# Seven block products in place of eight for ten pairs of row blocks of a down projection, its columns in two chunks

## The chip, the cores and the metric

One core of a Trainium2 chip runs the whole layer as one program. The metric is the device time in microseconds. Engines: PE does the matmuls (and loads their stationary operands, PEld), DVE the elementwise work on two operands, ACT copies and activations, SP issues most transfers, and POOL is all but idle here. Each engine works through its own instructions in order; they wait for each other by semaphores.

## What is computed

A layer with three attention branches and a gated MLP, in fp32, on 256 rows of 2048 columns. The part that changes is the last line, the down projection:

```python
h2 = _rmsnorm(x, ffn_norm)
u = _causal_dwconv(h2 @ w_up, conv_w, conv_b)
g, val = jnp.split(u, 2, axis=-1)
return x + (jax.nn.silu(g) * val) @ w_down    # (256 x 5504) @ (5504 x 2048)
```

## The kernel before

All weights come in the order of use as tiles of 128 x 1024 (512 KB), in an order that `weight_chunks` writes out by hand and the host packs. `w_tiles` loads a tile on SP's queue into one of four `raw` buffers (L155), rounds it on ACT to `whi` (L159) and subtracts on DVE to get the rest, `wlo` (L160); there are three buffers each of `whi` and `wlo`. The rounding and the subtraction have high priority. The order of the instructions on each engine is set by a scheduler when the program is built: what is ready first comes first, and the source order and the priority decide between what is ready. Pools hand out a buffer again when all that used it is done.

Activations are kept the same way, as a rounded part and a rest, and a product takes three matmuls: high by high, high by low, low by high. All go through `mm` (L100). The results are summed in PSUM, which has eight banks of 512 fp32 columns: pool `pj` has two tiles of two banks, pool `pa` the tiles `t`, `s` (twice) and `o` of a bank each.

The up stage goes over the 43 blocks of 128 hidden columns in pairs (the last one alone). For each pair and each half (gate, value) `proj_cols` takes 16 row blocks of `w_up`; then come the convolution on ACT and DVE, silu, the product of the halves (L820), and `split` into `fc` (L190, L192), which holds the hidden activations, transposed.

The down stage goes over `DOWN`: three chunks of 512 columns and two of 256. For each, `proj_rows` goes over the 43 row blocks of `w_down`, and for each row block over the two halves `tt` of the 256 rows, with three matmuls; the row blocks of one tile come together (two at 512 columns, four at 256). At the end of a chunk a piece of `x2d` (the residual, in DRAM) is loaded into `xr` on SP (L827), the sum is added on DVE (L828) and stored on SP's or ACT's queue (L829).

Of the kernel before, what the change touches and what calls it, by code (L numbers as in the profile page):

```python
# [11 lines left out]
F32 = mybir.dt.float32  # L12
F32R = mybir.dt.float32r
BF16 = mybir.dt.bfloat16
I32 = mybir.dt.int32
AF = mybir.ActivationFunctionType
# [3 lines left out]
P = 128  # L20
D = 2048
# [4 lines left out]
NFF = DFF // P  # L26
# [13 lines left out]
NEG = -1.0e30  # L40


DOWN = ((0, 512), (512, 512), (1024, 512), (1536, 256), (1792, 256))


def weight_chunks():

    for c in range(4):
        yield "kv", KD, c * 512, 512
    for base, n in ((QM, 1024), (KB, 1024), (QB, 1024), (VB, 512), (QI, 256), (QI + 256, 328), (VB + 512, 512)):  # L50
        for c in range(0, n, 512):
            yield "in", KD, base + c, min(512, n - c)
    for br in (2, 1, 0):
        for c in range(0, D, 512):
            yield "in", KD, GL + br * D + c, 512
            yield "b%d" % br, D // 2 // P, c, 512
        if br == 2:
            for base, n in ((KA, 256), (QA, 256), (VA, 512)):
                for c in range(0, 1024, n):
                    yield "in", KD, base + c, n  # L60
    for c in range(4):
        yield "out", KD, c * 512, 512
    for c in range(0, DFF, 256):
        for half in range(2):
            yield "up", KD, half * DFF + c, min(256, DFF - c)
    for c0, n in DOWN:
        yield "down", NFF, c0, n


def weight_tiles():  # L70
# [16 lines left out]
def hybrid_block(ctx: ExitStack, tc: tile.TileContext, x, xT, mem, memT, pos, inv, prm, gqk, bg, wts, out):  # L87
# [11 lines left out]
    def mm(o, l, r, start, stop):  # L99
        nc.tensor.matmul(o, l, r, start=start, stop=stop, skip_group_check=True)  # L100
# [44 lines left out]

    tiles = enumerate(weight_tiles())

    def w_tiles(name, nk, c0, n):

        j = 0  # L150
        while j < nk:
            at, (name_, j_, kn, c0_, n_) = next(tiles)
            assert (name_, j_, c0_, n_) == (name, j, c0, n), (name, j, c0, n)
            raw = wraw.tile([P, 1024], F32, name="raw")
            nc.sync.dma_start(raw[:, :kn * n], wts[at, :, :kn * n])  # L155
            hi = whl.tile([P, 1024], F32R, name="whi")
            lo = whl.tile([P, 1024], F32R, name="wlo")
            with tc.high_priority():
                nc.scalar.activation(hi[:, :kn * n], raw[:, :kn * n], AF.Copy)  # L159
                nc.vector.tensor_sub(lo[:, :kn * n], raw[:, :kn * n], hi[:, :kn * n].bitcast(F32))  # L160
            for k in range(kn):
                yield j + k, hi[:, k * n:(k + 1) * n], lo[:, k * n:(k + 1) * n]
            step()
            j += kn
# [625 lines left out]
        r2b = bcast_cols(const, r2, "r2b")  # L790


    with ExitStack() as fctx:
        ap_ = fctx.enter_context(tc.tile_pool(name="ap", bufs=1))
        up = fctx.enter_context(tc.tile_pool(name="up", bufs=2))
        fc = ap_.tile([P, NFF, 2, T], F32R, name="fc")
        for c0 in range(0, NFF, 2):
            nb = min(2, NFF - c0)
            conv = []
# [18 lines left out]
            g_, v_ = conv[0][:, :nb, :], conv[1][:, :nb, :]  # L818
            nc.scalar.activation(g_, g_, AF.Silu)
            nc.vector.tensor_mul(v_, g_, v_)  # L820
            split(fc[:, c0:c0 + nb], v_)

        for c0, n in DOWN:
            ps = proj_rows(fc, "down", NFF, c0, n)
            for tt in range(2):
                xr = up.tile([P, 512], F32, name="xr2")[:, :n]
                nc.sync.dma_start(xr, x2d[tt * P:(tt + 1) * P, c0:c0 + n])  # L827
                nc.vector.tensor_add(xr, xr, ps[:, tt, :n])  # L828
                (nc.sync, nc.scalar)[tt].dma_start(out[tt * P:(tt + 1) * P, c0:c0 + n], xr)  # L829


_ORDER = ["x", "xT", "mem", "memT", "pos", "inv", "prm", "gqk", "bg", "wts"]
# [39 lines left out]
```

## Time and profile before

| what | us |
|---|---|
| median of 3 runs (lowest, highest) | 1701.38 (1698.99, 1701.79) |
| the profiled execution, its own time | 1699.5 |
| the profiled execution, its span | 1697.8 |
| up stage, by the timeline of PE | 985 to 1456.4 |
| down stage, first matmul to last adds | 1456.5 to 1694.1 |

The span goes from the first to the last instruction of the profiled execution. The granted clock is 1.00 in all 40 slices of the page. Durations of matmuls overlap, since they are pipelined: their pace is read from their starts. In a row of a timeline a group of like instructions is merged (xcount), and square brackets tell how long the engine was idle before it and who released it.

### The profile page before, as it was taken

What the parts mean: (1) busy time and instruction counts of PE and PEld (TensorE: products, weight loads), DVE (VectorE), ACT (ScalarE), POOL (GpSimd) and SP (SyncE); (2) the same over time, 40 slices, a digit from 0 to 9 for tenths busy, and PEclk for the clock granted to TensorE, in tenths of its full rate; (3) what the DMA queues carried; (4) which work ended last, traced back from release to release, by engine and by line L of the source; (5) the groups of instructions that cost most, each with busy time, mean ns of one, the idle gap of its engine ahead of it and who ended that gap; (6) DMA issues with size and microseconds to landing.
All of it is one profiled execution on the core that took longest, in us unless ns stands there. A gap on an engine that the chain in (4) does not pass through costs nothing.

```text
span 1697.8 us, 22795 instructions
## 1 busy us (share of the span) xinstructions
PE 1686.8 (99%) x8658; PEld 1440.5 (85%) x8658; DVE 1071.7 (63%) x1589; ACT 863.5 (51%) x1147; POOL 6.9 (0%) x58
## 2 busy tenths in 40 slices
PE   8999999999999999999999999999999999999999
PEld 6888889888888888888888888888888888888899
DVE  6686866686554455555565577777777777644443
ACT  6555554444444477544444455555555555433432
POOL 0000000000000000000000000000000000000000
PEclk9999999999999999999999999999999999999999
DMA  9855445555565555566666665555555555565663
GB/s 329 299 186 188 144 155 180 180 186 184 176 199 190 195 174 173 183 211 203 203 203 218 218 210 190 192 190 187 193 191 187 191 193 187 193 205 204 220 205 128
DMA packets 99966, 332.80 MB, mean 196 GB/s; under 512 B 11152, under 2 KB 16656, under 8 KB 99856
## 3 DMA queue, kind: packets, MB, share of 16 engines
q1 hardware_dynamic: 98992, 330.29, 58.9%
q8 instruction: 67, 1.10, 0.2%
q10 hardware_dynamic: 864, 1.06, 0.2%
q14 instruction: 43, 0.35, 0.1%
HBM read 327.11 MB, written 4.19 MB: 195 GB/s over the span
## 4 chain that ended last, share of the span: by engine, by line
PE 99%; DMA 0%; DVE 0%; issue 0%; ACT 0%; SPq 0%; DVEq 0%
PE pj L100 95%; PE s L100 2%; PE o L100 1%; DMA raw<-in_wts 0%; PE t L554 0%; PE t L775 0%; PE t L749 0%; PE t L325 0%; PE t L676 0%; ACT whi L159 0%; DVE xf L369 0%; DVE wlo L160 0%; PE t L502 0%; DVE xc L192 0%; SPq L288 0%
## 5 line engine op out<-in xcount | busy, mean ns | idle before, releaser
L160 DVE TENSOR_TENSOR wlo<-raw,whi 128x1024 fp32r<-128x1024 f32 (+2 forms) x591 | 719.6, 1218 | 566.2 <-ACT whi L159 565.1
L159 ACT ACTIVATE whi<-raw 128x1024 fp32r<-128x1024 f32 (+2 forms) x591 | 623.3, 1055 | 778.8 <-PE pj L100 635.0
L100 PE MATMUL pj<-whi,xc 128*128 128x512 f32 (+2 forms) x1536 | 481.1, 387 | 0.5 <-DVE xc L192 0.5
L100 PE MATMUL pj<-x2c,whi 128*128 128x512 f32 x1376 | 477.4, 391 | 0.0
L100 PE MATMUL pj<-x2c,wlo 128*128 128x256 f32 x1376 | 385.5, 280 | 0.0
L100 PEld LDWEIGHTS pj<-whi,xc 128*128 128x128 f32 x1536 | 285.2, 188 | 55.3 <-DVE xc L192 1.0
L100 PEld LDWEIGHTS pj<-x2c,whi 128*128 128x128 f32 x1376 | 257.3, 187 | 56.3
L100 PE MATMUL pj<-wlo,xc 128*128 128x512 f32 (+2 forms) x768 | 293.3, 382 | 0.0
L100 PEld LDWEIGHTS pj<-x2c,wlo 128*128 128x128 f32 x1376 | 260.1, 189 | 0.0
L100 PE MATMUL pj<-whi,fc 128*128 128x512 f32 (+1 forms) x860 | 220.8, 347 | 0.0
L100 PEld LDWEIGHTS pj<-whi,fc 128*128 128x128 f32 x860 | 150.6, 189 | 20.2
L100 PEld LDWEIGHTS pj<-wlo,xc 128*128 128x128 f32 x768 | 144.6, 188 | 25.8
L100 PE MATMUL pj<-wlo,fc 128*128 128x512 f32 (+1 forms) x430 | 149.1, 347 | 0.0
L100 PEld LDWEIGHTS pj<-wlo,fc 128*128 128x128 f32 x430 | 81.4, 189 | 10.1
L100 PE MATMUL pj<-xc,whi 128*128 128x512 f32 x256 | 88.9, 394 | 0.0
L100 PE MATMUL pj<-whi,mc 128*128 128x512 f32 x256 | 81.8, 398 | 6.1 <-ACT whi L159 6.1
L100 PE MATMUL pj<-whi,mg 128*128 128x512 f32 x256 | 81.1, 393 | 0.0
L100 PE MATMUL pj<-xc,wlo 128*128 128x256 f32 x256 | 70.9, 277 | 0.0
L100 PEld LDWEIGHTS pj<-whi,mc 128*128 128x128 f32 x256 | 49.1, 192 | 16.3 <-ACT whi L159 6.3
L100 PEld LDWEIGHTS pj<-xc,whi 128*128 128x128 f32 x256 | 48.0, 188 | 11.1
L100 PEld LDWEIGHTS pj<-whi,mg 128*128 128x128 f32 x256 | 48.1, 188 | 9.8
L100 PE MATMUL pj<-wlo,mc 128*128 128x512 f32 x128 | 51.2, 400 | 0.4 <-DVE wlo L160 0.4
(222 smaller groups left out, 1297.1 us busy)
## 6 DMA issues: line engine op xcount, KB each, us to landing
raw<-in_wts SPq DMA_DIRECT2D x578, 512.0 KB, 3.3
th<-in_bg SPq DMA_DIRECT2D x24, 256.0 KB, 5.6
raw<-in_wts SPq DMA_DIRECT2D x5, 492.0 KB, 4.2
nat_rows<-in_mem SPq DMA_DIRECT2D x4, 512.0 KB, 6.5
nat_rows<-in_x SPq DMA_DIRECT2D x4, 512.0 KB, 6.9
xf<-in_xT SPq DMA_DIRECT2D x4, 512.0 KB, 5.3
xrow<-in_x SPq DMA_DIRECT2D x8, 256.0 KB, 4.4
x2d<-xrow SPq DMA_DIRECT2D x8, 256.0 KB, 4.2
```

The source lines that it names most:

```text
L100: nc.tensor.matmul(o, l, r, start=start, stop=stop, skip_group_check=True)
L159: nc.scalar.activation(hi[:, :kn * n], raw[:, :kn * n], AF.Copy)
L160: nc.vector.tensor_sub(lo[:, :kn * n], raw[:, :kn * n], hi[:, :kn * n].bitcast(F32))
```

## The change

The down projection's columns come as two chunks of 1024. Of the 43 row blocks, 20 pairs (a, b) and a tail of three blocks are taken. Ten of the pairs (`SEVEN`) take seven block products: rows of the pair's activations are halved by `tt` and its weights by column halves, which gives a 2 x 2 by 2 x 2 block product, in Winograd's form of Strassen's algorithm. The sums of the activation blocks are made in the up stage and kept in `sx` (three per pair) and in the place of a21 in `fc`; the sums of the weight blocks (`t`, then `th_` as high and low) are made in the down stage on DVE and ACT. Four of the seven products are summed over all pairs in banks of their own (`p1`, `p5`, `p6`, `p7`) and three go to the cells of the output (`cc`), where the other ten pairs and the tail add their plain products. `gather` adds the four sums to `e`, which starts as the residual from `x2d`; `store` adds a cell to `e` and sends it out. In the tail the cells are done one after the other, and the last cell of the last chunk in two halves of 256 columns. The pool `up` is closed before the down stage and the pool `dn` takes its place; the scratch for DMA descriptors goes from its standard size to 8192 bytes.

```diff
--- before.py
+++ after.py
@@ -40,7 +40,9 @@
 NEG = -1.0e30
 
 
-DOWN = ((0, 512), (512, 512), (1024, 512), (1536, 256), (1792, 256))
+
+SEVEN = (2, 3, 5, 7, 8, 10, 12, 13, 15, 17)
+TAIL = 3
 
 
 def weight_chunks():
@@ -63,8 +65,8 @@
     for c in range(0, DFF, 256):
         for half in range(2):
             yield "up", KD, half * DFF + c, min(256, DFF - c)
-    for c0, n in DOWN:
-        yield "down", NFF, c0, n
+    for c0 in range(0, D, 1024):
+        yield "down", NFF, c0, 1024
 
 
 def weight_tiles():
@@ -145,14 +147,18 @@
 
     tiles = enumerate(weight_tiles())
 
-    def w_tiles(name, nk, c0, n):
-
-        j = 0
+    def w_raw(name, j, c0, n):
+
+        at, (name_, j_, kn, c0_, n_) = next(tiles)
+        assert (name_, j_, c0_, n_) == (name, j, c0, n), (name, j, c0, n)
+        raw = wraw.tile([P, 1024], F32, name="raw")
+        nc.sync.dma_start(raw[:, :kn * n], wts[at, :, :kn * n])
+        return raw, kn
+
+    def w_tiles(name, nk, c0, n, j=0):
+
         while j < nk:
-            at, (name_, j_, kn, c0_, n_) = next(tiles)
-            assert (name_, j_, c0_, n_) == (name, j, c0, n), (name, j, c0, n)
-            raw = wraw.tile([P, 1024], F32, name="raw")
-            nc.sync.dma_start(raw[:, :kn * n], wts[at, :, :kn * n])
+            raw, kn = w_raw(name, j, c0, n)
             hi = whl.tile([P, 1024], F32R, name="whi")
             lo = whl.tile([P, 1024], F32R, name="wlo")
             with tc.high_priority():
@@ -790,10 +796,15 @@
         r2b = bcast_cols(const, r2, "r2b")
 
 
+
+
+
     with ExitStack() as fctx:
         ap_ = fctx.enter_context(tc.tile_pool(name="ap", bufs=1))
-        up = fctx.enter_context(tc.tile_pool(name="up", bufs=2))
         fc = ap_.tile([P, NFF, 2, T], F32R, name="fc")
+        sx = ap_.tile([P, len(SEVEN), 3, 2, P], F32R, name="sx")
+        uctx = ExitStack()
+        up = uctx.enter_context(tc.tile_pool(name="up", bufs=2))
         for c0 in range(0, NFF, 2):
             nb = min(2, NFF - c0)
             conv = []
@@ -818,15 +829,127 @@
             g_, v_ = conv[0][:, :nb, :], conv[1][:, :nb, :]
             nc.scalar.activation(g_, g_, AF.Silu)
             nc.vector.tensor_mul(v_, g_, v_)
+            if c0 // 2 in SEVEN:
+                i = SEVEN.index(c0 // 2)
+                st = conv[0].rearrange("p a t -> p (a t)")[:, :3 * P].rearrange("p (s t) -> p s t", t=P)
+                a11, a21, a12, a22 = (v_[:, b, tt * P:(tt + 1) * P] for b in range(2) for tt in range(2))
+                nc.vector.tensor_add(st[:, 0], a21, a22)
+                nc.vector.tensor_sub(st[:, 1], st[:, 0], a11)
+                nc.vector.tensor_sub(st[:, 2], a21, a11)
+                nc.vector.tensor_sub(a21, a12, st[:, 1])
+                split(sx[:, i], st)
             split(fc[:, c0:c0 + nb], v_)
-
-        for c0, n in DOWN:
-            ps = proj_rows(fc, "down", NFF, c0, n)
+        uctx.close()
+
+        dn = fctx.enter_context(tc.tile_pool(name="dn", bufs=1))
+        th_ = xp.tile([P, 2, 2, 4, 512], F32R, name="thl", tag="xc")
+        turn_ = [0]
+
+        def mm3(o, l, r, start, stop):
+
+            mm(o, l[0], r[0], start, False)
+            mm(o, l[0], r[1], False, False)
+            mm(o, l[1], r[0], False, stop)
+
+        def hl(t):
+            return t[:, 0, :], t[:, 1, :]
+
+        for c0 in range(0, D, 1024):
+            last = c0 + 1024 == D
+            e = dn.tile([P, 2, 2, 512], F32, name="e")
             for tt in range(2):
-                xr = up.tile([P, 512], F32, name="xr2")[:, :n]
-                nc.sync.dma_start(xr, x2d[tt * P:(tt + 1) * P, c0:c0 + n])
-                nc.vector.tensor_add(xr, xr, ps[:, tt, :n])
-                (nc.sync, nc.scalar)[tt].dma_start(out[tt * P:(tt + 1) * P, c0:c0 + n], xr)
+                nc.sync.dma_start(e[:, tt], x2d[tt * P:(tt + 1) * P, c0:c0 + 1024])
+            cc = [pj.tile([P, 2, 512], F32, name="pj") for _ in range(2)]
+            p1, p5, p6, p7 = (pa.tile([P, 512], F32, name=nm, bufs=nb) for nm, nb in
+                              (("t", 1), ("s", 2), ("s", 2), ("o", 1)))
+            begun = set()
+
+            def add(key, o, l, r, stop):
+                mm3(o, l, r, key not in begun, stop)
+                begun.add(key)
+
+            def eight(k, hi, lo, cells, cols=(0, 512)):
+                for tt, h in cells:
+                    r = tuple(w[:, h * 512 + cols[0]:h * 512 + cols[1]] for w in (hi, lo))
+                    add((tt, h), cc[tt][:, h, cols[0]:cols[1]], hl(fc[:, k, :, tt * P:(tt + 1) * P]), r,
+                        k == NFF - 1)
+
+            cells = [(tt, h) for tt in range(2) for h in range(2)]
+
+            def seven(p):
+                a, b = 2 * p, 2 * p + 1
+                i, end = SEVEN.index(p), p == SEVEN[-1]
+                ra, rb = (w_raw("down", k, c0, 1024)[0] for k in (a, b))
+                ha, hb = (whl.tile([P, 1024], F32R, name="whi") for _ in range(2))
+                la, lb = (whl.tile([P, 1024], F32R, name="wlo") for _ in range(2))
+                t = dn.tile([P, 4, 512], F32, name="t")
+                tq = th_[:, turn_[0] % 2]
+                turn_[0] += 1
+                b11, b12, b21, b22 = ra[:, :512], ra[:, 512:], rb[:, :512], rb[:, 512:]
+                with tc.high_priority():
+                    nc.scalar.activation(ha[:, :512], b11, AF.Copy)
+                    nc.scalar.activation(hb, rb, AF.Copy)
+                    nc.vector.tensor_sub(t[:, 0], b12, b11)
+                    nc.vector.tensor_sub(t[:, 1], b12, b22)
+                    nc.vector.tensor_sub(t[:, 2], b22, t[:, 0])
+                    nc.vector.tensor_sub(t[:, 3], b21, t[:, 2])
+                    nc.vector.tensor_sub(la[:, :512], b11, ha[:, :512].bitcast(F32))
+                    nc.vector.tensor_sub(lb, rb, hb.bitcast(F32))
+                    for q in range(2):
+                        th, tl = tq[:, 0, 2 * q:2 * q + 2], tq[:, 1, 2 * q:2 * q + 2]
+                        nc.scalar.activation(th, t[:, 2 * q:2 * q + 2], AF.Copy)
+                        nc.vector.tensor_sub(tl, t[:, 2 * q:2 * q + 2], th.bitcast(F32))
+                step()
+                w11 = ha[:, :512], la[:, :512]
+                w21, w22 = ((hb[:, h], lb[:, h]) for h in (slice(0, 512), slice(512, 1024)))
+                w1, w3, w2, w4 = (hl(tq[:, :, q]) for q in range(4))
+                s1, s2, s3 = (hl(sx[:, i, q]) for q in range(3))
+                a11, s4 = (hl(fc[:, a, :, tt * P:(tt + 1) * P]) for tt in range(2))
+                a12, a22 = (hl(fc[:, b, :, tt * P:(tt + 1) * P]) for tt in range(2))
+                add("p1", p1, a11, w11, end)
+                add((0, 0), cc[0][:, 0], a12, w21, False)
+                add((0, 1), cc[0][:, 1], s4, w22, False)
+                add("p5", p5, s1, w1, end)
+                add("p7", p7, s3, w3, end)
+                add("p6", p6, s2, w2, end)
+                add((1, 0), cc[1][:, 0], a22, w4, False)
+
+            def gather():
+
+                u = wraw.tile([P, 1024], F32, name="raw")[:, :512]
+                nc.vector.tensor_add(e[:, 0, 0], e[:, 0, 0], p1)
+                nc.scalar.activation(u, p6, AF.Copy)
+                nc.vector.tensor_add(u, u, p1)
+                for tt in range(2):
+                    nc.vector.tensor_add(e[:, tt, 1], e[:, tt, 1], p5)
+                nc.vector.tensor_add(e[:, 0, 1], e[:, 0, 1], u)
+                nc.vector.tensor_add(u, u, p7)
+                nc.vector.tensor_add(e[:, 1], e[:, 1], u.unsqueeze(1).to_broadcast([P, 2, 512]))
+
+            def store(tt, a, b):
+                d = e[:, tt].rearrange("p h n -> p (h n)")[:, a:b]
+                nc.vector.tensor_add(d, d, cc[tt].rearrange("p h n -> p (h n)")[:, a:b])
+                (nc.sync, nc.scalar)[tt].dma_start(out[tt * P:(tt + 1) * P, c0 + a:c0 + b], d)
+
+            for p in range((NFF - TAIL) // 2):
+                if p in SEVEN:
+                    seven(p)
+                    if p == SEVEN[-1]:
+                        gather()
+                else:
+                    for k, hi, lo in w_tiles("down", 2 * p + 2, c0, 1024, 2 * p):
+                        eight(k, hi, lo, cells)
+            rest = list(w_tiles("down", NFF, c0, 1024, NFF - TAIL))
+            for tt, h in cells:
+                if last and (tt, h) == cells[-1]:
+                    for a in (0, 256):
+                        for k, hi, lo in rest:
+                            eight(k, hi, lo, [(tt, h)], (a, a + 256))
+                        store(tt, h * 512 + a, h * 512 + a + 256)
+                else:
+                    for k, hi, lo in rest:
+                        eight(k, hi, lo, [(tt, h)])
+                    store(tt, h * 512, h * 512 + 512)
 
 
 _ORDER = ["x", "xT", "mem", "memT", "pos", "inv", "prm", "gqk", "bg", "wts"]
@@ -861,7 +984,7 @@
         "bg": c(np.asarray(b_gate).reshape(1, 3 * D)),
         "wts": wts,
     }
-    nc = bacc.Bacc("TRN2", target_bir_lowering=False, num_devices=1)
+    nc = bacc.Bacc("TRN2", target_bir_lowering=False, num_devices=1, dynamic_dma_scratch_size=8192)
     args = [nc.dram_tensor(f"in_{n}", arrays[n].shape, mybir.dt.from_np(arrays[n].dtype), kind="ExternalInput").ap()
             for n in _ORDER]
     out = nc.dram_tensor("out_0", (T, D), F32, kind="ExternalOutput").ap()
```

## Rows read from the trace of the kernel before

**Rows 1.** The page: busy us (share of span) xinstructions of each engine; the chain, by line.

```profile
PE 1686.8 (99%) x8658; PEld 1440.5 (85%) x8658; DVE 1071.7 (63%) x1589; ACT 863.5 (51%) x1147; POOL 6.9 (0%) x58
...
PE pj L100 95%; PE s L100 2%; PE o L100 1%; DMA raw<-in_wts 0%; PE t L554 0%; PE t L775 0%; PE t L749 0%; PE t L325 0%; PE t L676 0%; ACT whi L159 0%; DVE xf L369 0%; DVE wlo L160 0%; PE t L502 0%; DVE xc L192 0%; SPq L288 0%
```

**Rows 2.** Two stretches (up, down): length, busy us (xinstructions), PEclk, DMA share, GB/s.

```profile
985.00:1456.40 471.40, 471.40 (x2722) 415.60 (x2721) 355.27 (x469) 268.46 (x343) 4.37 (x44) 1.00 0.57 191
...
1456.40:1694.10 237.70, 237.64 (x1292) 207.22 (x1290) 110.93 (x104) 90.92 (x90) 0.00 (x0) 1.00 0.59 194
```

**Rows 3.** Timeline of PE: start us, us of the merged matmuls, engine, line, operation, tiles.

```profile
1456.49 0.39 PE L100 MATMUL pj<-whi,fc 128*128 128x512 f32 x1
...
1599.78 0.62 PE L100 MATMUL pj<-whi,fc 128*128 128x512 f32 x2
...
1600.46 0.62 PE L100 MATMUL pj<-whi,fc 128*128 128x512 f32 x2
...
1633.16 0.28 PE L100 MATMUL pj<-wlo,fc 128*128 128x256 f32 x1
...
1633.52 0.28 PE L100 MATMUL pj<-wlo,fc 128*128 128x256 f32 x1
```

**Rows 4.** PE's groups in the down stage, by shape: xcount, busy us, mean ns.

```profile
L100 PE MATMUL pj<-whi,fc 128*128 128x512 f32 x516 | 158.9, 389 | 0.0
L100 PE MATMUL pj<-wlo,fc 128*128 128x512 f32 x258 | 100.4, 389 | 0.0
L100 PE MATMUL pj<-whi,fc 128*128 128x256 f32 x344 | 62.1, 283 | 0.0
L100 PE MATMUL pj<-wlo,fc 128*128 128x256 f32 x172 | 48.7, 283 | 0.0
```

**Rows 5.** Timeline of DVE at the end of the up stage.

```profile
1447.76 0.68 DVE L806 TENSOR_TENSOR u<-pj,u 128x512 f32<-128x512 f32 x1
1448.48 0.69 DVE L807 TENSOR_TENSOR u<-u,r2b 128x512 f32<-128x512 f32 x1
...
1452.16 1.22 DVE L160 TENSOR_TENSOR wlo<-raw,whi 128x1024 fp32r<-128x1024 f32 x1
1453.31 0.68 DVE L820 TENSOR_TENSOR cv<-cv,cv 128x512 f32<-128x512 f32 x1
1453.91 0.42 DVE L806 TENSOR_TENSOR u<-pj,u 128x256 f32<-128x256 f32 x1
...
1464.45 0.42 DVE L192 TENSOR_TENSOR fc<-cv,fc 128x256 fp32r<-128x256 f32 x1
```

**Rows 6.** DVE's and ACT's groups by shape, whole run: xcount, busy us, mean ns, idle.

```profile
L192 DVE TENSOR_TENSOR ac<-e,ac 128x384 fp32r<-128x384 f32 x8 | 4.4, 555 | 2.4 <-ACT ac L190 2.4
...
L160 DVE TENSOR_TENSOR wlo<-raw,whi 128x512 fp32r<-128x512 f32 x5 | 3.5, 693 | 5.7 <-ACT whi L159 5.7
...
L465 DVE TENSOR_TENSOR nat<-rt 128x128 f32<-128x128 f32 x4 | 1.1, 283 | 0.0
...
L159 ACT ACTIVATE whi<-raw 128x1024 fp32r<-128x1024 f32 x578 | 612.8, 1060 | 757.8 <-PE pj L100 615.9 <-issue 90.6 <-ACT cv L811 32.1
```

**Rows 7.** Timeline of ACT and DVE, a steady stretch of the down stage.

```profile
1674.64 1.06 ACT L159 ACTIVATE whi<-raw 128x1024 fp32r<-128x1024 f32 x1 [1.82 <-PE pj L100]
...
1675.73 1.23 DVE L160 TENSOR_TENSOR wlo<-raw,whi 128x1024 fp32r<-128x1024 f32 x1 [1.66 <-ACT whi L159]
```

**Rows 8.** Timeline of DVE where one chunk of the down projection ends.

```profile
1516.09 0.68 DVE L828 TENSOR_TENSOR xr<-xr,pj 128x512 f32<-128x512 f32 x1
1516.68 1.22 DVE L160 TENSOR_TENSOR wlo<-raw,whi 128x1024 fp32r<-128x1024 f32 x1
```

**Rows 9.** DMA issues of the down stage (KB, us to landing); the loads of tile xr.

```profile
raw<-in_wts SPq DMA_DIRECT2D x83, 512.0 KB, 3.3
...
L827 SPq DMA_DIRECT2D xr<-x2d x10: 326/326/427, 985.0 to 1668.3; - x10
```

**Rows 10.** Timeline of DVE at the end of the run.

```profile
1694.08 0.75 DVE L828 TENSOR_TENSOR xr<-xr,pj 128x256 f32<-128x256 f32 x2 [6.08 <-PE pj L100]
```

## The prediction

> **What bounds the kernel now.** I read the page's busy line first, then the chain that ended last. PE is busy 99% of the span, and the chain is PE's own matmuls for 95% of it [rows 1]; no other engine is near it (DVE 63%, ACT 51%). So only fewer or cheaper matmuls, or a shorter end, can save anything, and every other edit counts only where it makes PE wait. The stretches show the same for the stage that changes: in the down projection PE is busy for all of its 237.7 us, while DVE works 111 us and ACT 91 [rows 2]. The stage begins with the matmul at 1456.49 and ends when the last adds start at 1694.08 [rows 3, 10]: 237.6 us.
>
> The recorded duration of a matmul overlaps the next one, so I take the pace from starts. Three matmuls of 512 columns start every 0.68 us (1599.78 to 1600.46), three of 256 every 0.36 (1633.16 to 1633.52) [rows 3]: 226.7 and 120 ns each. The stage holds 516 + 258 = 774 of the first and 344 + 172 = 516 of the second [rows 4]. 774 x 0.2267 + 516 x 0.120 = 175.4 + 61.9 = 237.4, so counts times pace give the stage to 0.2 us, and I use them for the new kernel.
>
> **Matmuls, the gain.** Each chunk of 1024 columns has 43 row blocks; a plain row block takes 4 cells x 3 = 12 wide matmuls, a pair 24, a seven-product pair 21. Per chunk: 23 x 12 + 10 x 21 = 486, so 972 in all. The last cell of the last chunk is cut in two, so 9 of these become 18 narrow ones: 963 x 0.2267 + 18 x 0.120 = 218.3 + 2.2 = 220.5 us. The saving is 237.4 - 220.5 = 16.9 us: 60 products fewer make 13.6, and joining narrow matmuls into wide ones makes 3.3. The new products have the shapes of the old, so nothing speaks for another pace. This is the ceiling.
>
> **DVE and ACT in a seven pair.** A plain pair asks DVE for two 1024-wide subtractions; a seven pair asks for five of 512 (t0 to t3, la) and three of 1024 (lb, and one for each half of the sums). The trace prices these twice. By starts, back to back: 1452.16 to 1453.31 is 1.15 for 1024, 1453.31 to 1453.91 is 0.60 for 512, and 1447.76 to 1448.48 is 0.72 for 512 when the next one needs its result [rows 5], as t3 needs t2. So 4 x 0.60 + 0.72 + 3 x 1.15 = 6.57 us. By recorded durations, 0.69 for 512 [rows 6] and 1.23 for 1024 [rows 5], it is 5 x 0.69 + 3 x 1.23 = 7.1. PE needs only 21 x 0.2267 = 4.76 us for such a pair. A plain pair is the opposite: DVE 2.3 (2.45), PE 5.44.
>
> So what counts is the dense stretch, pairs 2 to 17, with ten seven pairs and six plain: PE 10 x 4.76 + 6 x 5.44 = 80.2 us; DVE 65.7 + 13.8 = 79.5 by starts, 71 + 14.7 = 86 by durations. DVE is the equal of PE there. By starts nothing is lost if DVE never idles; by durations 5.8 us a chunk, 11.6 in all. I take the price by starts, because these operations stand back to back as those in [rows 5] do, and add 1.5 us a chunk for moments in which DVE has to wait, since 0.7 us of slack in 80 covers little: waits for ACT's rounded copies, for a hi buffer that PE still reads (three of them, a pair takes two), for the single t tile. 3 us in all, between 0 and 12. ACT has four copies a pair, none wider than the 1.06 of [rows 6]: at most 4.2 us, not the bound.
>
> The row above shows DVE starting an operation 0.08 us before the recorded end of the one in front. The Trainium skill's page "VectorE: DVE Perf Modes", section "The DRAIN you can't avoid", says that the next operation does not start until the pipe is empty (and refers to another section for operations that nothing holds). By it the 7.1 would hold, and the stretch would lose 11.6 us; by the row it loses nothing. That is the second case below.
>
> **The sums of the activations.** In the up stage ten block pairs get four operations of 128 columns (0.283) and a split of 384 (DVE 0.555) [rows 6]: 4 x 0.29 + 0.56 = 1.7 us of DVE each, 17 in all. DVE is busy 355 of 471 us there and PE all of it [rows 2], and the weight subtractions have priority, so I cost this at nothing; without that cover it is 17 us.
>
> **Seams.** A weight tile is ready 1.06 (copy) + 1.23 (subtraction) = 2.3 us after its buffer comes free [rows 7]. In the tail three tiles are held at once. Block 42 gets its buffer when PE starts block 40, and its lo is needed seven matmuls later, 1.59 us: a stall of 0.7 to 0.8 a chunk. The next chunk's first tile gets its buffer six matmuls (1.36 us) before the chunk ends and its lo is due one matmul after: 2.3 - 1.36 - 0.23 = 0.7. Behind it PE's third cell needs the PSUM tile that the last store's add still reads; in the kernel before, such an add ran ahead of the next weight subtraction (1516.09, then 1516.68) [rows 8], and if here two subtractions went first it would cost some 1.8 more. At the very end the first half's add reads the bank that the second half's matmuls write: one add and two handoffs, 0.5, and in return one narrow add in place of two behind the last matmul, -0.3 (both adds take 0.75) [rows 10]. I take 1.6 + 1.0 + 0.2 = 2.8 us, between 1.6 and 5.
>
> **Queues.** The loads of e stand in the source ahead of the chunk's weights, on SP, and the first must wait until the up stage's tiles are dropped. But the queue isn't in source order: the loads of xr stand behind the loop over the weights, and the first was issued at 985.0 [rows 9], half a millisecond ahead. So I expect e where it hinders nothing: 0, with the third case as its other end. gather takes one of the four raw buffers for its u, from the end of pair 17 until its chain of some 5.5 us is through; a load takes 3.3 us to land [rows 9] and then 2.3. If the loads go round in strict order, the fourth tile behind pair 17 comes at 5.5 + 3.3 + 2.3 = 11.1 and is due 3 x 2.72 = 8.2 us on: 3 us a chunk. If any free buffer is taken, nothing; I take 0 and keep 6 for the range. gather's and the stores' adds fall between plain tiles, where DVE has 1.5 us free in each 2.7. The smaller scratch for DMA descriptors touches no queue that carries these loads.
>
> **The sum.** 220.5 + 3 + 2.8 = 226.3 against 237.6: 11.3 us saved. The profiled execution took 1699.5 (span 1697.8); the median of the runs is 1701.4, 1.9 above. So 1688.2 by the one and 1690 by the other, which I predict.
>
> **The cases.**
> - Forecast, 0.62: PE's count decides, with 3 to 10 us of stalls; 1686 to 1696, likeliest 1690.
> - DVE becomes the bound in the dense stretch, 0.20. For it: 79.5 against 80.2 leaves no slack, and at the recorded durations it is 86. Against it: the starts in [rows 5]. Price 11.6 + 4 of seams: 220.5 + 15.6 = 236.1, 1.5 us saved: 1700, with 1697 to 1702 about it.
> - Slower: e's load stands at the head of SP's queue while the up stage's last tiles are still in use, 0.07. The last of their work (1464.45 [rows 5]) ends some 8 us into the stage; then the load, 3.3 us of landing and 2.3 of splitting follow, while what is already loaded lasts at most a few tiles, or nothing: up to 14 us of idle PE. 1690 + 14 = 1704. It decides against the change once the tiles in hand run out more than 11 us before the next one; [rows 9] speak against it.
> - u's buffer holds up the loads, 0.05: 6 us, 1696.
> - The change does more: no shortfall of DVE, small seams, 0.06: 220.5 + 1.6, 1685 to 1686.
>
> The range runs from 1685 (fewest stalls) to 1701 (DVE as the bound). A measurement of this kernel tells about 0.2%, 3.4 us, from no change. Faster than that takes in the first, fourth and fifth case and a third of the second: 0.79; within it 0.14; slower 0.07.
>
> **What would show it.** Right: down-stage matmuls of 963 and 18 at 226.7 and 120 ns; idle PE in the stage of 4 to 8 us, most of it at the blocks 42 and at the start of the second chunk; DVE busy over 90% between the first and the last seven pair of a chunk; the up stage as long as before. Wrong: idle PE before nearly every seven pair, released by DVE's lo or tl (then DVE is the bound and its price by starts was too low); a gap of many us at the start of the stage with SP waiting (the third case); an up stage that grew; or a pace other than 226.7.

## The result

The changed kernel takes 1710.45 us (1710.18 to 1713.12) against 1701.2 us before: ratio 1.0060, 95% interval 1.0043 to 1.0078. It is slower by some 9 us, where 1690 was predicted. Its profiled execution took 1710.57 us, with a span of 1708.8.

In some executions of several kernels here, the one before included, the up stage alone runs some 9 us longer (the last section shows its pace); times below are those of the other executions, with their lowest and highest, while ratios are over all executions.

The page of the changed kernel, first busy us (share of the span) of each engine, then the chain by engine, beside [rows 1]:

```profile
PE 1682.8 (98%) x8349; PEld 1419.3 (83%) x8349; DVE 1175.5 (69%) x1770; ACT 897.0 (52%) x1197; POOL 6.9 (0%) x58
...
PE 94%; DVE 3%; DMA 2%; issue 1%; ACT 0%; SPq 0%; DVEq 0%; ACTq 0%
```

PE has 309 matmuls fewer, but is only 4.0 us less busy, and DVE and DMA now stand on the chain. The stretches say where. Columns: length, then busy us (x instructions) of PE, PEld, DVE, ACT and POOL, granted clock, DMA share, GB/s; the up stage, the down stage, and four pieces of the latter:

```profile
985.98:1457.38 471.40, 471.40 (x2722) 415.65 (x2721) 368.92 (x519) 272.70 (x353) 4.20 (x41) 1.00 0.58 190
1457.38:1705.50 248.12, 232.29 (x983) 185.07 (x981) 201.48 (x235) 120.25 (x130) 0.00 (x0) 0.97 0.57 188
1482.00:1545.00 63.00, 63.00 (x280) 52.02 (x279) 62.47 (x74) 37.93 (x41) 0.00 (x0) 1.00 0.64 210
...
1555.00:1565.00 10.00, 8.24 (x29) 6.67 (x30) 5.41 (x6) 2.12 (x2) 0.00 (x0) 0.83 0.71 226
1595.00:1605.00 10.00, 7.60 (x25) 5.35 (x24) 7.43 (x9) 5.58 (x6) 0.00 (x0) 0.83 0.86 308
1675.00:1685.00 10.00, 6.09 (x20) 4.28 (x19) 7.99 (x9) 3.43 (x4) 0.00 (x0) 0.74 0.31 99
```

The up stage is as long as before [rows 2]. The down stage is 248.1 us instead of 237.7, with PE idle for 15.8 of it, where it was never idle. The dense stretch of seven pairs, 1482 to 1545, has no idle PE at all. The loss sits in short pieces, and in three of them the granted clock is below 1.

PE's matmuls of the down stage by shape (xcount, busy us, mean ns, idle before), beside [rows 4]:

```profile
L102 PE MATMUL pj<-whi,fc 128*128 128x512 f32 x442 | 146.8, 399 | 4.9 <-ACT whi L165 2.1 <-ACT whi L891 1.6 <-DVE e L931 1.2
L102 PE MATMUL pj<-wlo,fc 128*128 128x512 f32 x221 | 89.1, 403 | 8.7 <-DVE wlo L166 7.4 <-DVE wlo L897 1.2
L102 PE MATMUL s<-thl,sx 128*128 128x512 f32 x120 | 36.0, 399 | 0.6 <-ACT thl L900 0.5
L102 PE MATMUL o<-thl,sx 128*128 128x512 f32 x60 | 18.1, 400 | 0.0
L102 PE MATMUL pj<-thl,fc 128*128 128x512 f32 x60 | 17.5, 389 | 0.0
...
```

With the 60 that go into tile t, 442 + 221 + 120 + 60 + 60 + 60 = 963, as counted ahead; the 18 narrow ones are there too. To see what they lost I went through the starts in order and summed what each distance has above 0.2267 us, wherever it is more than 0.1 above. That is 26.2 us in all, against the 5.8 of the prediction:

| stretch | us lost |
|---|---|
| start of the stage, the first seven pairs (1460 to 1482) | 3.0 |
| behind pair 17, first chunk (1551 to 1561) | 6.0 |
| end of the first chunk and start of the second (1571 to 1581) | 2.8 |
| first seven pairs of the second chunk (1591 to 1605) | 5.2 |
| one gap at 1648 | 0.5 |
| behind pair 17, second chunk (1676 to 1687) | 6.7 |
| end of the run | 2.1 |

So 13 us lie where `gather` stands, 8 where `e` is loaded, 5 at the seams.

**Behind pair 17.** The timeline of PE, then ACT, then DVE of the changed kernel there (start, us, engine, line, operation; in brackets the idle time before and its releaser):

```profile
1551.27 0.84 PE L102 MATMUL pj<-thl,fc 128*128 128x512 f32 x3
1553.07 0.73 PE L102 MATMUL pj<-whi,fc 128*128 128x512 f32 x2 [0.95 <-ACT whi L165]
1556.76 0.66 PE L102 MATMUL pj<-wlo,fc 128*128 128x512 f32 x1 [2.96 <-DVE wlo L166]
1557.22 1.06 PE L102 MATMUL pj<-whi,fc 128*128 128x512 f32 x2
1558.07 0.63 PE L102 MATMUL pj<-wlo,fc 128*128 128x512 f32 x1
1558.50 0.63 PE L102 MATMUL pj<-whi,fc 128*128 128x512 f32 x1
...
1551.47 0.60 ACT L921 ACTIVATE raw<-s 128x512 f32<-128x512 f32 x1 [5.69 <-PE s L102]
1551.97 2.94 ACT L165 ACTIVATE whi<-raw 128x1024 fp32r<-128x1024 f32 x3
...
1550.11 1.28 DVE L924 TENSOR_TENSOR e<-e,s 128x512 f32<-128x512 f32 x2 [1.35 <-PE s L102]
1552.10 0.69 DVE L922 TENSOR_TENSOR raw<-raw,t 128x512 f32<-128x512 f32 x1 [0.70 <-ACT raw L921]
...
1554.34 1.23 DVE L927 TENSOR_TENSOR e<-e,raw 128x1024 f32<-128x1024 f32 x1
1555.49 3.49 DVE L166 TENSOR_TENSOR wlo<-raw,whi 128x1024 fp32r<-128x1024 f32 x3
```

ACT's copy of p6 (L921) can't run before p6's last matmul. ACT stands at it for 5.69 us, with the roundings (L165) of the next three plain blocks behind it in the queue; they come within 2.94 us, once it is through. DVE is held in the same way: the additions of `gather`, of which L922 waits for that copy, stand ahead of the three subtractions of those blocks (L166), which end the gap of 2.96. And once PE is back, its matmuls start every 0.43 us in place of 0.2267, a ratio of 1.9: the lower of the engine's two levels, 1.2 GHz instead of 2.4, in a stretch with a granted clock of 0.83. So the two gaps cost 4.2 us by the starts (3.9 of it idle, 0.95 and 2.96), and some 1.8 of slow matmuls follow. The second chunk repeats it (gaps 4.2, slow matmuls 2.5, clock 0.74).

**Where e is loaded.** SP's timeline at the start of the stage:

```profile
1465.41 0.80 SPq L861 DMA_DIRECT2D e<-x2d  x2
1466.70 18.21 SPq L155 DMA_DIRECT2D raw<-in_wts  x7
```

The groups of DMA issues from 1462 to 1476 (KB each, us to landing):

```profile
raw<-in_wts SPq DMA_DIRECT2D x3, 512.0 KB, 7.1
e<-x2d SPq DMA_DIRECT2D x2, 512.0 KB, 7.3
```

What ACT waited for from 1457 to 1485 (us in total, times, longest):

```profile
ACT whi L165 <- DMA raw<-in_wts: 4.6, 2, 4.5
```

`e` is loaded at the start of its chunk and not ahead as `xr` was [rows 9]; the raw loads beside it land after 7.1 us instead of 3.3, ACT waits for them, and PE for ACT and DVE.

In the second chunk the first load of `e` also waits on SP's queue for the store of the first chunk, with the raw loads behind it (SP's waits: us in total, times, longest):

```profile
SPq L861 <- DMA out<-e: 7.4, 1, 7.4
```

Slow matmuls follow there too: between 1601 and 1605 seven start 0.41 to 0.43 us apart, in the window with a granted clock of 0.83 above. With their neighbours they make some 1.7 of the 5.2 us.

**Seams.** PE's timeline at the end of the first chunk and at the end of the run:

```profile
1576.75 0.50 PE L102 MATMUL pj<-whi,fc 128*128 128x512 f32 x1 [1.15 <-DVE e L931]
...
1580.17 0.50 PE L102 MATMUL pj<-wlo,fc 128*128 128x512 f32 x1 [0.77 <-DVE wlo L166]
...
1702.37 0.39 PE L102 MATMUL pj<-whi,fc 128*128 128x256 f32 x1 [1.15 <-DVE e L931]
...
1704.21 0.39 PE L102 MATMUL pj<-whi,fc 128*128 128x256 f32 x1 [0.51 <-DVE e L931]
```

Only the second and the last were forecast. The two of 1.15 are those of the last cell, (1, 1): it waits for the store's add of cell (1, 0), whose sums lie in the same PSUM tile.

### The profile page after: what moved, and what is told of

Its sections match the earlier page's. It is cut to its first block, busy times and chain, and to the rows that moved or that the text cites. A ratio compares the mean times of both kernels' runs of the same rounds, so it can differ in the third digit from the quotient of the medians.

```text
span 1708.8 us, 22370 instructions
## 1 busy us (share of the span) xinstructions
PE 1682.8 (98%) x8349; PEld 1419.3 (83%) x8349; DVE 1175.5 (69%) x1770; ACT 897.0 (52%) x1197; POOL 6.9 (0%) x58
## 4 chain that ended last, share of the span: by engine, by line
PE 94%; DVE 3%; DMA 2%; issue 1%; ACT 0%; SPq 0%; DVEq 0%; ACTq 0%
PE pj L102 88%; PE s L102 3%; PE o L102 2%; DMA raw<-in_wts 1%; DVE wlo L166 1%; PE t L102 1%; DMA out<-e 0%; ACT whi L165 0%; PE t L560 0%; PE t L781 0%; DVE t L893 0%; DVE e L931 0%; PE t L755 0%; PE t L331 0%; PE t L682 0%
## 5 line engine op out<-in xcount | busy, mean ns | idle before, releaser
L166 DVE TENSOR_TENSOR wlo<-raw,whi 128x1024 fp32r<-128x1024 f32 (+1 forms) x549 | 669.0, 1220 | 453.4 <-ACT whi L165 452.4
L165 ACT ACTIVATE whi<-raw 128x1024 fp32r<-128x1024 f32 (+1 forms) x549 | 579.0, 1057 | 686.1 <-PE pj L102 539.7
L102 PE MATMUL pj<-whi,fc 128*128 128x512 f32 (+1 forms) x454 | 149.5, 397 | 6.6 <-DVE e L931 2.8
L102 PEld LDWEIGHTS pj<-whi,fc 128*128 128x128 f32 x454 | 86.5, 192 | 28.2 <-DVE e L931 4.4
L102 PE MATMUL pj<-wlo,fc 128*128 128x512 f32 (+1 forms) x227 | 90.8, 400 | 8.7 <-DVE wlo L166 7.4
L900 ACT ACTIVATE thl<-t 128x1024 fp32r<-128x1024 f32 x40 | 42.2, 1056 | 39.2 <-DVE t L893 32.5
L102 PEld LDWEIGHTS pj<-wlo,fc 128*128 128x128 f32 x227 | 43.9, 193 | 20.6 <-DVE wlo L166 9.5
```

What stands on the lines that cost most here:

```text
L900: nc.scalar.activation(th, t[:, 2 * q:2 * q + 2], AF.Copy)
```

## The experiments

My theory after the result: the seven products themselves give what was counted and DVE keeps up, and the three kinds of stalls above take it away. The rivals were the wide chunks, DVE, and, for single stalls, other causes in the same place. The kernel before, timed again beside each of the three series of experiments, took 1700.7, 1700.4 and 1701.3 us; the changed kernel was timed in one series only, beside 1701.2. So a microsecond between two series says nothing.

**Wide chunks alone.** No seven pairs, so no `gather`; the rest as in the changed kernel.

```diff
-SEVEN = (2, 3, 5, 7, 8, 10, 12, 13, 15, 17)
+SEVEN = ()
```

> Part of the change alone: the two chunks of 1024 columns, e, the cells one after the other in the tail, but every pair takes its eight products; no sums, no gather. Theory (what is lost is lost in queues: gather's instructions in front of the next weight tiles, and e's loads in front of the raw loads at the start of a chunk; DVE is not the bound): PE's work is 234.1 us against 237.4, the seams take back 3 to 5, e's loads 0 to 5, so 1700 to 1708, and no idle PE at pair 17. Rival (the loss is DVE's work for the seven products): nearly all of the changed kernel's 26 us of idle PE is gone and it ends near 1701 - 3 = 1698 to 1700.

Measured: 1703.1 us (1701.6 to 1703.8, nine of ten executions), beside 1700.7 before; ratio 1.0006 [0.9987, 1.0024]. Its starts lose 5.0 us, all at the four seams; at the start of both chunks, where it loads the same `e`, there is nothing. So the chunks cost some 2 us and aren't the loss: they give the 3.3 us of joined matmuls and take 5.0 at the seams. And a megabyte of `e` costs nothing as long as the blocks around it are plain.

**gather behind the next blocks.** The instructions of `gather` are queued behind the roundings and subtractions of the next plain blocks, up to block 38; u stays in a raw buffer.

```diff
-                    if p == SEVEN[-1]:
-                        gather()
 ...
                         eight(k, hi, lo, cells)
+                        if k == GATHER_AFTER:      # 38
+                            with tc.issue_after(seen["act"]), tc.issue_after(seen["dve"]):
+                                gather()
```

> The changed kernel, but gather's instructions on ACT and DVE are queued behind the rounding and the subtraction of row block 38 (three blocks after pair 17) instead of wherever they are first ready. Theory (gather stands at the head of ACT's and DVE's queues and waits for PE while the next tiles wait behind it; the two idle stretches then also cost clock): both stretches go, 6.2 and 6.7 us, and little comes in their place: 1697 to 1700. Rival (DVE has too much to do, and its backlog shows wherever it is heavy): gather's 5 us of DVE work are only moved and the idle time moves with them: 1706 to 1711.

Measured: 1696.4 us (1695.7 to 1698.9, five of ten), 14 less than the changed kernel and a little under what I expected. Both stretches behind pair 17 are gone, and the slow matmuls there with them. Slow matmuls remain where `e` is loaded: in the profiled execution, the slowest of the five, six and seven of them start 0.43 us apart at the starts of the two chunks, and these places lose 4.3 and 4.4 us.

**e later.** The two halves of `e` are loaded behind the raw loads ahead of pairs 5 and 10.

```diff
-            for tt in range(2):
-                nc.sync.dma_start(e[:, tt], x2d[tt * P:(tt + 1) * P, c0:c0 + 1024])
 ...
+                if p in (5, 10):
+                    with tc.issue_after(seen["sp"]):
+                        nc.sync.dma_start(e[:, p // 10], x2d[p // 10 * P:(p // 10 + 1) * P, c0:c0 + 1024])
```

> The changed kernel, but the two loads of e (512 KB each) are queued on SP behind the raw loads ahead of pairs 5 and 10, not at the start of the chunk. Theory (the loads of e stand in front of the raw loads that the first pairs need, by 512 KB each on the same DMA queue and, in the second chunk, by a wait for the stores): the 3.4 us of idle PE in the first 25 us and about 5 us at the start of the second chunk go, in all 6 to 8 us: 1702 to 1705. Rival (the first seven pairs wait for DVE, which still has the up stage's last work to do): the first stretch stays, and less than 3 us are won: 1707 to 1711.

Measured: 1704.9 us (1704.0 to 1705.3, five of ten), 5.6 less than the changed kernel, at the upper end of what I expected. The starts of the two chunks lose 0.7 and 1.2 us where they lost 3.0 and 5.2; `gather`'s stretches stay at 6.0 and 7.1.

**Both.** The two edits together.

> Both moves together. Theory: the two causes are separate, so the gains add: 1710.5 - 12.9 - 7 = 1690.6, between 1688 and 1694, and what is left idle is the seams (blocks 42, the second chunk's first tile, the last bank), some 5 us. Rival (DVE is the bound of the dense pairs): the gains don't add, since each only uncovers DVE, and the time stays over 1697.

Measured: 1692.0 us (1690.8 to 1692.9, three of ten), 18.5 less; the two gains, 14.0 and 5.6, all but add up. The starts lose 6.9 us, close to the 5.8 forecast, and the time is 2 us from the 1690 predicted. That closeness is partly luck: the seams take 5.0 in place of 2.8, the rest some 2 in place of 3.

**Does DVE have room?** The kernel with both edits, with the last of the four subtractions for t done twice in each seven pair.

```diff
                     nc.vector.tensor_sub(t[:, 3], b21, t[:, 2])
+                    nc.vector.tensor_sub(t[:, 3], b21, t[:, 2])
```

> Both moves together, and in every seven pair one 512-wide subtraction on DVE (t3) is done twice. Theory (in the dense stretch DVE's 79.5 us stand against PE's 80.2, priced by starts, so there is no room): 10 x 0.60 to 0.72 = 6 to 7 us more of DVE a chunk, of which all but a little slack comes out as idle PE in the dense stretch: 8 to 13 us more in the two chunks. Rival (the buffers hide it, DVE has real room): under 2 us more.

Measured: 1702.7 us (1701.8 to 1704.0), 10.7 more than without. PE's waits for what the seven pairs need, in its down stage (us in total, times, longest):

```profile
PE s L103 <- ACT thl L901: 2.1, 4, 0.8
PE s L103 <- DVE thl L902: 1.2, 3, 0.5
```

A window between the first and last seven pairs of this kernel, and the same of the kernel with both edits alone:

```profile
1490.00:1550.00 60.00, 57.83 (x247) 45.16 (x246) 57.06 (x69) 32.78 (x36) 0.00 (x0) 1.00 0.61 207
```

```profile
1490.00:1550.00 60.00, 60.00 (x265) 49.24 (x264) 59.53 (x69) 37.01 (x40) 0.00 (x0) 1.00 0.68 221
```

In the first PE is idle for 2.2 us, before seven pairs, released by what ACT and DVE make of t; in the second it is never idle, with DVE busy for 59.53 of 60. Twenty more operations of 0.60 us are 12; the stage grew by 9.8 (228.5 to 238.3 from first to last start). So most of the added work comes out as time. By the difference DVE had some 1.1 us of room a chunk, beside the 0.7 of the prediction (80.2 against 79.5), but that is an estimate: in the first window DVE itself idles for 2.9 us, 2.2 of them waiting for ACT's copies of t. The added operation also makes this chain from DVE to ACT and back longer, and no run tells the two apart.

**The order of the tail.** Both edits, and the four cells of the tail go (0, 0), (1, 0), (0, 1), (1, 1): first the left half of both PSUM tiles, then the right.

```diff
-            for tt, h in cells:
+            for tt, h in sorted(cells, key=lambda c: c[1]):
```

> Both moves together, and in the tail the four cells come as (0,0), (1,0), (0,1), (1,1), so that two cells in a row lie in different PSUM tiles. Theory (the add of a finished cell holds back the matmuls into the other bank of the same tile, 1.3 us of idle PE in each tail with both moves): 2 to 2.6 us less than with both moves alone, at the same pace of the up stage. Rival (PE waits there for weights, or DVE is late): no change within 0.7 us.

Measured: 1688.0 us (1687.0 to 1689.4), ratio to before 0.9928 [0.9913, 0.9943]: the best version, faster than both kernels; the kernel before took 1700.4 beside it. What PE still waits for in the whole down stage:

```profile
PE pj L103 <- DVE wlo L168: 0.8, 1, 0.8
PE pj L103 <- DVE e L931: 0.5, 1, 0.5
PE s L103 <- DVE thl L901: 0.4, 1, 0.4
PE pj L103 <- DVE wlo L897: 0.3, 1, 0.3
```

The add (L931) was waited for 2.8 us in three places, now 0.5 in one. From first to last start the down stage is 2.9 us shorter (228.5 to 225.6), most of it those waits. The times differ by 3.9, but they come from two series, and the other microsecond isn't in this stage.

**A shorter tail.** The version above with one row block in the tail instead of three.

```diff
-TAIL = 3
+TAIL = 1
```

> Both moves and the swapped cells, and a tail of one row block in place of three (the other two make one more plain pair). Theory (three tiles held at once cost 0.7 to 0.8 for block 42's late buffer and 0.7 to 1.0 for the second chunk's first tile): those stalls go, the adds (0.6 each) just keep up with cells of 0.68, and the last add comes later by at most 0.6: 1 to 2 us less than with the swapped cells alone. Rival (the adds of four cells now stand behind one another and hold the PSUM tiles of the next chunk): 0 to 2 us more.

Measured: 1690.3 us (1690.2 to 1694.8), 2.3 more, so what I expected fell. Not all of it is the tail: between the profiled executions, 3.3 us apart, the down stage is 0.9 us longer from first to last start (225.6 to 226.5) and what follows the last start 0.5, while 1.8 us lie ahead of the stage, where nothing was changed. PE waits 1.9 us for the adds, three times up to 0.8: with three matmuls to a cell in place of nine, the next cell of the same PSUM tile comes before the add is through, in the swapped order too.

**Is it u's buffer, or the order?** The changed kernel, with nothing but a buffer of its own for u.

```diff
-                u = wraw.tile([P, 1024], F32, name="raw")[:, :512]
+                u = dn.tile([P, 512], F32, name="u")
```

> The changed kernel, with gather's u in a buffer of its own in place of one of the four raw buffers; gather's place in the queues is left as it is. Theory (gather's instructions stand at the head of ACT's and DVE's queues): the idle stretch behind pair 17 stays, at least 10 of the 13 us: 1708 to 1711 at the pace of the up stage that the changed kernel had. Rival (u takes away a raw buffer and the loads come late): the stretch goes, 1697 to 1700.

Measured: 1696.6 us (1695.2 to 1698.5), 13.9 less, ratio to before 0.9978 [0.9969, 0.9987]. My theory, the order of the queues, had given 1708 to 1711 and missed; the rival, the buffer, had it. But ACT's timeline in this kernel shows that the edit had moved the order too:

```profile
1547.64 3.05 ACT L165 ACTIVATE whi<-raw 128x1024 fp32r<-128x1024 f32 x3 [1.66 <-PE pj L102]
1551.67 0.60 ACT L921 ACTIVATE u<-s 128x512 f32<-128x512 f32 x1 [0.98 <-PE s L102]
```

The three roundings now stand ahead of the copy, without a word on order in the edit. The run didn't tell the two apart. The next did: u in its own buffer, and blocks 36 to 38 queued behind the copy and the last addition.

```diff
-            with tc.high_priority():
+            with ExitStack() as order_:
+                order_.enter_context(tc.high_priority())
+                if name == "down" and 2 * SEVEN[-1] + 2 <= j <= 2 * SEVEN[-1] + 4:   # 36 to 38
+                    for ins in front[-2:]:          # the copy of p6, the last add to e
+                        order_.enter_context(tc.issue_after(ins))
                 nc.scalar.activation(hi[:, :kn * n], raw[:, :kn * n], AF.Copy)
 ...
-                nc.scalar.activation(u, p6, AF.Copy)
+                front.append(nc.scalar.activation(u, p6, AF.Copy).ins)
```

> The changed kernel with gather's u in a buffer of its own, and the splits into hi and lo of blocks 36 to 38 queued behind gather's ACT copy and its last DVE addition. If the stretch of idle TensorE behind the seven pairs comes from the order of the ACT and DVE queues (the splits of the plain blocks behind gather's copy and additions), it returns in spite of u's own buffer: idle gaps of 1 to 4 us beside block 36 in both chunks, followed by matmuls at the lower clock, and 1707 to 1711 us. If it comes from the occupied raw buffer (the rival), the time stays that of u in its own buffer, 1695 to 1699, with no gap beside block 36. By the slower pace of the up stage both would be 9 us more.

Measured: 1709.8 us (1707.1 to 1712.3, eight of ten), 13.2 more than with u's own buffer alone. ACT and PE in this kernel:

```profile
1550.11 0.60 ACT L926 ACTIVATE u<-s 128x512 f32<-128x512 f32 x1 [5.69 <-PE s L102]
1550.60 2.94 ACT L170 ACTIVATE whi<-raw 128x1024 fp32r<-128x1024 f32 x3
...
1551.70 0.73 PE L102 MATMUL pj<-whi,fc 128*128 128x512 f32 x2 [0.95 <-ACT whi L170]
1555.39 0.50 PE L102 MATMUL pj<-wlo,fc 128*128 128x512 f32 x1 [2.95 <-DVE wlo L171]
```

The 5.69, the 0.95 and the 2.95 are those of the changed kernel, and the slow matmuls follow. Four kernels now make a square:

| us lost behind pair 17, both chunks | gather ahead in the queues | gather behind |
|---|---|---|
| u in a raw buffer | 6.0 and 6.7 (the change) | nothing (gather behind the next blocks) |
| u in its own buffer | 6.0 and 5.9 | nothing |

The order makes the loss, the buffer doesn't. What the buffer does is done when the program is built: with u in the raw pool the scheduler put `gather` ahead, with u outside it behind. Why it chose so was not measured.

**What of e costs?** The changed kernel, with `e` loaded from ACT's queue, so that SP's raw loads pass it:

```diff
-                nc.sync.dma_start(e[:, tt], x2d[tt * P:(tt + 1) * P, c0:c0 + 1024])
+                nc.scalar.dma_start(e[:, tt], x2d[tt * P:(tt + 1) * P, c0:c0 + 1024])
```

> The changed kernel with the two loads of e issued from ACT's queue instead of SP's. If the gaps at the start of both chunks come from SP's queue standing behind e's loads (the raw loads behind them issue late), the raw loads issue when their buffers come free and the gaps fall away: 5 to 8 us less than the changed kernel, 1702 to 1706. If they come from the megabyte itself, which shares the DMA engines with the raw loads whichever queue issues it, the raw loads still land 3 us or more late and the time stays within 3 us of the changed kernel, 1708 to 1712. By the slower pace of the up stage both would be 9 us more.

and with half of `e` at the chunk's start, the other half behind the raw load ahead of pair 10:

```diff
-            for tt in range(2):
-                nc.sync.dma_start(e[:, tt], x2d[tt * P:(tt + 1) * P, c0:c0 + 1024])
+            nc.sync.dma_start(e[:, 0], x2d[0:P, c0:c0 + 1024])
 ...
+                if p == 10:
+                    with tc.issue_after(seen["sp"]):
+                        nc.sync.dma_start(e[:, 1], x2d[P:2 * P, c0:c0 + 1024])
```

> The changed kernel with only the first token tile of e loaded at each chunk's start (half a megabyte), the second half behind the raw load of pair 10. If the amount loaded ahead of the first raw blocks sets the gaps, they shrink to half or less: the first stretch from 3.4 to at most 1.7 us, the second chunk's from 5 to at most 2.5, 3 to 6 us less in all, 1704 to 1708. If a place in the queue ahead of the raw loads is what costs, whatever the amount, they stay at 3.4 and 5 us and the time at 1709 to 1712. By the slower pace of the up stage both would be 9 us more.

Measured: 1709.6 us (1708.1 to 1712.6, nine of ten) and 1705.4 (1705.1 to 1706.1, six of ten). The raw loads of the first seven pairs (the groups of DMA issues over the same 14 or 15 us), from ACT's queue, with half of `e`, and with `e` later:

```profile
raw<-in_wts SPq DMA_DIRECT2D x4, 512.0 KB, 4.8
e<-x2d ACTq DMA_DIRECT2D x2, 512.0 KB, 5.6
```

```profile
raw<-in_wts SPq DMA_DIRECT2D x5, 512.0 KB, 4.1
e<-x2d SPq DMA_DIRECT2D x1, 512.0 KB, 5.1
```

```profile
raw<-in_wts SPq DMA_DIRECT2D x4, 512.0 KB, 3.2
```

In order, the first stretch loses 2.6, 0.6 and 0.7 us, and the second chunk's 3.8, 1.7 and 1.2; the changed kernel 3.0 and 5.2. A queue of its own hardly helps the first stretch, though the second half of `e` went out only at 1472.5 there, 6.7 us later than on SP; half the amount does help. So it is the megabyte on the DMA engines at that time, not its place on SP. In the second chunk the ACT version isn't a clean answer, since there a rounding stood 3.8 us behind the load of `e`, which waited for the store of the chunk before. With half of `e` the load on SP still waits 6.2 us for that store, and 1.7 us are lost in place of 5.2: that wait alone doesn't make the loss either.

## Why the prediction was wrong

**Right: what bounds, and PE's count.** 963 and 18 matmuls, at 0.2267 and 0.12 us wherever nothing held them. Without what the starts lose, 247.8 - 26.2 = 221.6 us are left of the changed kernel's stage, where 220.5 were counted. The version with most of the stalls taken out is 12.3 us faster than the kernel before (1688.0 against 1700.4).

**Right: DVE priced by starts.** The dense stretch has PE at 63.00 of 63.00 and DVE at 62.47, and the second case (1700) is out. DVE's timeline in the changed kernel:

```profile
1507.88 0.68 DVE L893 TENSOR_TENSOR t<-raw 128x512 f32<-128x512 f32 x1
1508.48 0.68 DVE L894 TENSOR_TENSOR t<-raw,t 128x512 f32<-128x512 f32 x1
1509.19 0.69 DVE L895 TENSOR_TENSOR t<-raw,t 128x512 f32<-128x512 f32 x1
```

A start follows 0.60 us after that of the operation in front, and 0.71 where it needs that one's result, as [rows 5] had it. The Trainium skill's page "VectorE: DVE Perf Modes", section "The DRAIN you can't avoid", says that the next operation does not start until the pipe is empty. By recorded durations, as that rule would have it, the prediction came to a loss of 11.6 us; the stretch lost nothing. What holds here is the reservation in the same section, that an operation that nothing holds starts earlier.

**Right: the sums in the up stage.** 471.40 us before and after, with DVE at 368.9 instead of 355.3: hidden.

**Too small, and by other terms: the seams.** 2.8 us were forecast, 1.6 to 5; 5.0 were lost. The terms were not the right ones: block 42 stalls nowhere (1.6 forecast), the second chunk's first tile 0.8 (1.0 forecast), the last bank 0.5. What was missed is the last cell waiting for the add of its neighbour in the same PSUM tile, 1.15 in each chunk; I applied that handoff to the last bank alone, not to the two cells of one tile.

**Wrong: "gather's and the stores' adds fall between plain tiles, where DVE has 1.5 us free in each 2.7".** That step counted room on DVE and let the operations fall into it. They can't: an engine goes through its queue in order, and the scheduler had put them ahead of the next three blocks. ACT's copy was left out of the step altogether, though its wait for p6, the second last product of the pair, was to be read from the source. This term, put at 0, is 12.7 us, some 4 of them from matmuls at the lower clock behind the idle stretch, which no step of the prediction had at all. The fourth case looked at the right line (u in the raw pool), but priced it as a late load, 6 us, and not as an order of queues.

**Wrong: the loads of e at 0.** The third case had them at the head of SP's queue with up to 14 us of idle PE once the first tiles ran out. The wait was 0.5 us at most at the first chunk, so that case is out as described; what came is its smaller relative. (The 7.4 us of the second chunk, for the store of the first, stood in no case.) The megabyte came as the densest run of blocks began, and the raw loads beside it took twice as long. Measured: 8.2 us with what remains at these places, some 1.7 of it slow matmuls; 5.6 by the edit. The step had asked only where in the queue the load stands, not what it does to the loads beside it.

So the sum fails by two terms put at nothing. PE's 220.5 with the 26.2 us lost between starts, 12.7 and 8.2 of them in these two places, is 246.7, where 247.8 lie between the first start and the last.

## What to carry to other kernels

An operation that waits for the last product of a group, queued ahead of the splits that feed the next group, can stop the engine behind, however much room its own engine has (6 us a chunk here): look at its place in the queue, not at the busy share. A buffer borrowed from a busy pool can change that place when the program is built; so when an edit with one purpose moves the time by more than expected, compare the order of the instructions before believing its cause. A large load beside a run of blocks that need their own loads soon can delay those (here 7.1 us to landing in place of 3.3); between plain blocks the same load cost nothing, so put it there.

## What was unexpected

After the idle stretches behind pair 17 the next 8 to 11 matmuls started every 0.427 us; the granted clock of those windows was 0.83 and 0.74 and then 1.00 again. The gaps so cost half as much again there (4.3 us of slow matmuls to 8.4 of gaps).

The up stage has two paces. The same stretch of 100 us in an execution of the changed kernel, and in one with both edits (windows; the count of matmuls is the second number):

```profile
1300.00:1400.00 100.00, 100.00 (x579) 88.19 (x578) 79.04 (x113) 58.64 (x77) 0.92 (x9) 1.00 0.58 190
```

```profile
1300.00:1400.00 100.00, 100.00 (x568) 86.67 (x567) 78.68 (x114) 56.58 (x74) 0.93 (x9) 1.00 0.57 188
```

PE is never idle in either, and the granted clock is 1.00 in both, but the second does 568 matmuls where the first does 579. Matmuls of 512 and of 256 columns alternate there; a couple takes 353 ns instead of 347, from the start of the stage to its end, some 9 us in all. The down stage isn't touched: with both edits its wide matmuls start every 0.227 us, as in the changed kernel. The kernel before had the longer pace in some of its executions, so no edit here causes it. What decides it stays open.
